# One product of 512 columns for both halves of the activations in the second layer's mixer

## The chip, the cores and the metric

The kernel runs on one core of one Trainium2 chip. The metric is the device time in microseconds (us) of one execution, as the median of the runs. Everything called an engine below belongs to that one core: TensorE (PE, with its weight loads as PEld), VectorE (DVE), ScalarE (ACT), GpSimd (POOL) and SyncE (SP), which issues the transfers.

## The reference

Two layers of an encoder on 256 tokens of width 2048, in float32. The part that matters is the first half of a layer, the mixer (cut):

```python
h = rmsnorm(x, norm_mix[l]) * (1.0 + sc_a) + sh_a
qa, ka, va, qb, kb, vb, ga, gb = split_cols(h @ w_in[l])
...
ya = window_attention(qa, ka, va, sink_a[l]) @ w_proj_a[l]
...
yb = neighbourhood_attention(qb, kb, vb, rel_bias_b[l]) @ w_proj_b[l]
merged = jax.nn.sigmoid(ga) * ya + jax.nn.sigmoid(gb) * yb
x = x + gt_a * (merged @ w_out[l])

h = rmsnorm(x, norm_ffn[l]) * (1.0 + sc_m) + sh_m
u = depthwise_conv(h @ w_up[l], conv_w[l], conv_b[l])
g, v = jnp.split(u, 2, axis=-1)
x = x + gt_m * ((jax.nn.silu(g) * v) @ w_down[l])
```

The six modulation vectors (sc_a, sh_a, gt_a and the same for the second half) are `silu(c) @ ada_w[l] + ada_b[l]`, computed in the kernel as well.

## The kernel before

**Split numbers.** TensorE multiplies in a shortened format (fp32r). To keep float32 accuracy each weight block and each activation is kept as a high half and a low half (the remainder), and a product is the sum of three: high by high, high weight by low activation, low weight by high activation.

**Blocks.** Every weight is cut into blocks of 128 by 128, and each layer's blocks stand in one stream in the order of use. Sixteen blocks are a unit: one transfer of 1 MB (`w`). A unit is split in two pieces of eight blocks (`hl_<unit>_<piece>`): ACT casts the high half (L348), then DVE subtracts to get the low half (L349). There are four buffers for pieces, and four for what the transfers bring (`raw`), which units of weights and of the modulation matrix (`aw`) share. The modulation product is done on DVE (L248), one `aw` after the other, paced by a plan against the unit number.

**Products.** `features` multiplies a row of blocks with the 16 (or 8) chunks of the activations into one PSUM tile (`ps`, four of them in turn) and then calls an evacuation. For each block `feature_block` issues, in the narrow form, three products of 256 columns (L395, L396, L397). In the wide form the two halves of the activations lie so that one access reads both (`Wide`): high weights by both halves is one product of 512 columns (L391), low weights by the high half one of 256 (L392). The sum then lies in two parts in the PSUM tile, which the evacuation adds. Before, the wide form is used in the feed-forward part only (`BOTH_HALVES`).

**The second layer's mixer, stage by stage.** After the query, key and value columns (`tokens`), with units counted from 0 in the layer: the rest of gate a (units 44 to 51, evacuation `gate_a`), projection a of the window attention's output `oA` (units 52 to 59, `proj_a`), gate b (units 60 to 75, `gate_b`), projection b of `oB` (units 76 to 83, `merge`, which also makes the halves of `merged`), the out product of `merged` (units 84 to 99, `residual`, into x). The attention heads run beside them, paced by the units. In the out product the first three output chunks share one pass over `merged` (`OUT_TURNS`), so its first three PSUM tiles are open at once; the others follow one by one.

**What sets the order.** A scheduler orders each engine's instructions when the kernel is built, so an engine's queue need not follow the code. At run time each engine takes its queue strictly in that order.

The narrow and the wide form of a block before:

```python
if isinstance(act, Wide):
    nc.tensor.matmul(ps[:], hi, act.both, start=first, stop=False)
    nc.tensor.matmul(ps[:, :S], lo, act.high, start=False, stop=last)
    return
out = ps[:, : 2 * act[0].shape[1]]
nc.tensor.matmul(out, hi, act[0], start=first, stop=False)
nc.tensor.matmul(ps[:, :S], hi, act[1], start=False, stop=False)
nc.tensor.matmul(out, lo, act[0], start=False, stop=last)
```

Of the kernel before, what the change touches and what calls it, by code (L numbers as in the profile page):

```python
# [15 lines left out]
P = 128  # L16
L = 2
D = 2048
S = 256
# [66 lines left out]
SCORES_3 = (1,)  # L86
EARLY = {1: 2}

BOTH_HALVES = (0,1)

MOVED_QK = [(), (0,1,2,8)]
QK_STEPS = 3
# [53 lines left out]
def encoder(ctx: ExitStack, tc: tile.TileContext, a: dict, out: bass.AP):  # L146
# [252 lines left out]
    class Stream:  # L399
# [54 lines left out]
        def tokens(self, h, kcs):  # L454

            pss = [mm.tile([P, 512], F32, name=f"ps{self.l}_{self.u}_t{t}", tag="mm") for t in range(2)]
            for kc in kcs:
                for _ in range(4):
                    hl, j = self.next_block()
                j -= 3  # L460
                hi, lo = (turns(hl[:, i, j * P : (j + 4) * P]) for i in range(2))
                for t, ps in enumerate(pss):
                    xh, xl = (h[kc][:, i, t * P : (t + 1) * P] for i in range(2))
                    nc.tensor.matmul(ps[:], xh, hi, start=kc == kcs[0], stop=False)  # L464
                    nc.tensor.matmul(ps[:], xh, lo, start=False, stop=False)  # L465
                    nc.tensor.matmul(ps[:], xl, hi, start=False, stop=kc == kcs[-1])  # L466
                if self.l == 0 and self.u == 1 and self.at == 4:
                    warm(WARM_ROW)
                if self.at == UB:
                    self.tick()  # L470
            return [turned_back(ps[:]) for ps in pss]

    def split(dst, src, scale=None, held=False):

        if isinstance(dst, Wide):
            hi, lo = dst.halves
            nc.scalar.copy(hi, pair(src))
            nc.vector.tensor_tensor(out=lo, in0=pair(src), in1=hi.bitcast(F32), op=ALU.subtract)
            return
        if scale is None:  # L480
            high = nc.scalar.copy(dst[:, 0], src)
            if held:
                tc.keep_in_program_order(high)
            nc.vector.tensor_tensor(out=dst[:, 1], in0=src, in1=dst[:, 0].bitcast(F32), op=ALU.subtract)
            return
        nc.scalar.activation(out=dst[:, 0], in_=src, func=AF.Copy, scale=scale)
        nc.vector.scalar_tensor_tensor(
            out=dst[:, 1], in0=src, scalar=scale, in1=dst[:, 0].bitcast(F32), op0=ALU.mult, op1=ALU.subtract
        )
# [64 lines left out]
    def normed(l, w, h, rbs):  # L554

        mod, amod = mods[l], amods[l]
        for kc in range(KC):
            t = ev.tile([P, S], F32, name="ht", tag="z")
            sh = mod[:, 3 * w * KC + kc : 3 * w * KC + kc + 1]
            nc.vector.scalar_tensor_tensor(  # L560
                out=t[:], in0=x[:, kc], scalar=amod[:, w, kc : kc + 1], in1=rbs[:], op0=ALU.mult, op1=ALU.mult
            )
            src = t[:]
            if isinstance(h[kc], Wide):
                hi, lo = h[kc].turned()
                src = src.rearrange("p (q r) -> p q r", r=2)
            else:
                hi, lo = h[kc][:, 0], h[kc][:, 1]
                if w:
                    hi, lo, src = turns(hi), turns(lo), src.rearrange("p (q r) -> p q r", r=2)  # L570
            nc.scalar.activation(out=hi, in_=src, func=AF.Identity, bias=sh)  # L571
            nc.vector.scalar_tensor_tensor(  # L572
                out=lo, in0=src, scalar=sh, in1=hi.bitcast(F32), op0=ALU.add, op1=ALU.subtract
            )
            yield
# [6 lines left out]
    class Bare:  # L582
# [42 lines left out]
        def roots(self):  # L625
            self.rbs = spread(self.rs)
            self.h = led(f"h{self.l}_{self.w}")
            if self.w and self.l in BOTH_HALVES:
                self.h = [Wide(c) for c in self.h]
            self.steps = normed(self.l, self.w, self.h, self.rbs)  # L630
            bg.add(self.steps, H_RATE[self.w])
# [89 lines left out]
    def attend(q, k, v, p, mask, scale, sink, o, rows=None):  # L721

        sc = ax.tile([P, 2, S], F32, name="sc", tag="ax")
        for t in range(2):
            for i, j in by(q):
                key = turns(k[j]) if len(q) > 1 else k[j]
                nc.tensor.matmul(sc[:, t], q[i][:, t * P : (t + 1) * P], key, start=i + j == 0, stop=(i, j) == by(q)[-1])
        m = sm.tile([P, 2], F32, name="m", tag="m")
        for t in range(2):
            nc.vector.tensor_tensor_reduce(  # L730
                out=pair(p[:, t]) if len(q) > 1 else p[:, t], in0=turned_back(sc[:, t]) if len(q) > 1 else sc[:, t],
                in1=pair(mask[:, t]) if len(q) > 1 else mask[:, t], scale=scale, scalar=-3.0e38 if sink is None else sink,
                op0=ALU.add, op1=ALU.max, accum_out=m[:, t : t + 1],
            )
        nm = sm.tile([P, 2], F32, name="nm", tag="nm")
        nc.vector.tensor_scalar(out=nm[:], in0=m[:], scalar1=-1.0, scalar2=None, op0=ALU.mult)
        den = sm.tile([P, 2], F32, name="den", tag="den")
        for t in range(2):
            nc.scalar.activation(out=p[:, t], in_=p[:, t], func=AF.Exp, bias=nm[:, t : t + 1], accum_out=den[:, t : t + 1])
        if sink is not None:  # L740
            es = sm.tile([P, 2], F32, name="es", tag="es")
            nc.scalar.activation(out=es[:], in_=nm[:], func=AF.Exp, bias=sink)
            nc.vector.tensor_tensor(out=den[:], in0=den[:], in1=es[:], op=ALU.add)
        ri = sm.tile([P, 2], F32, name="ri", tag="ri")
        nc.vector.reciprocal(out=ri[:], in_=den[:])  # L745
        for t in range(2):
            nc.scalar.activation(out=p[:, t], in_=p[:, t], func=AF.Copy, scale=ri[:, t : t + 1])
        yield
        if rows is not None:
            turned_blocks(p[:], rows(), 2)  # L750
            for _ in range(STEPS[sink is None]):
                yield
            tp = p
        else:
            tp = ax.tile([P, 2, S], F32, name="tp", tag="ax")
            for k in range(2):
                for t in range(2):
                    nc.tensor.transpose(tp[:, k, t * P : (t + 1) * P], p[:, t, k * P : (k + 1) * P], ident[:])
        pT = at.tile([P, 2, 2, S], F32R, name="pT", tag="pT", bufs=1)
        split(pT, tp[:], held=rows is not None)  # L760
        v = v()
        yield
        po = ax.tile([P, 512], F32, name="po", tag="ax")
        for i, j in by(v):
            for b in range(2):
                nc.tensor.matmul(po[:, :S], v[i][:, b], turns(pT[:, j, b]), start=i + j + b == 0, stop=i + b == 2)
        o = o()
        src, hi, lo = turned_back(po[:, :S]), pair(o[:, 0]), pair(o[:, 1])
        nc.scalar.copy(hi, src)
        nc.vector.tensor_tensor(out=lo, in0=src, in1=hi.bitcast(F32), op=ALU.subtract)  # L770

# [120 lines left out]
    for l in range(L):  # L892
# [35 lines left out]
        kTa, qTa = packs[0][:, 0:3:2], packs[0][:, 4:12]  # L928
        kvs = [None, None]

        ready, heads = [0], [0]
        oA, oB = [], []

        def head_a(i):
            g = i // (HA // GA)
            if i >= 6:
                oA.append(paired(F32R, f"oA{l}_{i}", (i - 6) * (ROW - OFF)))
            elif i % 2 == 0:
                o = place(("y0", "y1", "y2")[i // 2], 4, F32R, f"oA{l}_{i}")
                oA.extend((o[:, :2], o[:, 2:]))  # L940
            q = in_halves(qTa[:, i], f"qA{l}_{i}", "qh", l in SCORES_3)
            if i % (HA // GA) == 0:
                kvs[0] = in_halves(kTa[:, g], f"kA{l}_{g}", "kh", l in SCORES_3)
# [29 lines left out]
        def oB_of(hb):  # L973
            if hb == 0:
                o = place("a", 12, F32R, f"oB{l}_{hb}")
                oB.extend(o[:, 2 * i : 2 * i + 2] for i in range(6))
            elif hb == 6:
                oB.extend(chunks_of(sp, "b0", 6, f"oB{l}_{hb}", 2))
            return oB[hb]

        def attention():
# [28 lines left out]
        for pi, (groups, gates) in enumerate(parts):  # L1010
# [38 lines left out]
            for mo in range(BARE[0] if l else 0, KC):  # L1049

                def gate_a(ps):
                    src, to = ps, pair(ya[:, mo])
                    if pi > 0:
                        nc.vector.tensor_tensor(out=to, in0=ps, in1=to, op=ALU.add)
                        src = to
# [11 lines left out]
        for mo in range(KC):  # L1067

            def proj_a(ps):
                gated(pair(ya[:, mo]), pair(ya[:, mo]), ps)  # L1070

            st.features(oA, [proj_a])
        if l:
# [8 lines left out]

        def gate_b(mo):
            def evac(ps):
                half_tanh(pair(gb[mo]), ps)

            return evac

        for mo in range(KC):
            st.features(hs, [gate_b(mo)])  # L1090
        bg.finish(job)
        merged = led(f"merged{l}")
        for mo in range(KC):

            def merge(ps):
                z = ev.tile([P, S], F32, name="m", tag="z")
                gated(pair(z[:]), pair(gb[mo]), ps)
                nc.vector.tensor_tensor(out=z[:], in0=z[:], in1=ya[:, mo], op=ALU.add)
                split(merged[mo], z[:], 0.5)

# [195 lines left out]
```

## Time and profile before

| | |
|---|---|
| median of 3 runs (lowest to highest) | 2586.07 us (2584.91 to 2586.75) |
| the profiled execution's own time | 2584.3 us |
| its span, first to last instruction | 2581.7 us |
| mean granted TensorE clock | 0.998 |
| second layer's mixer from the rest of gate a to the end of out | about 1560.7 to 1880.8 us of the span |

The profile gives, for the whole span and for any stretch of it, how long each engine was busy; a busy PE only says that some product was in flight. Rows of instructions have the start, the duration, engine, line, operation, output and input; the time in brackets behind a row is how long the engine had stood idle before it, and what ended that. On an engine with a pipeline the next instruction starts before the last one's duration is over, so the step from start to start is what an instruction takes away from the others.

### The profile page before, as it was taken

How to read it: one execution, taken by the hardware profiler on the slowest of the kernel's cores; microseconds unless marked ns; L12 is line 12 of the kernel's file. 1: busy time of each engine (PE TensorE's matmuls, PEld its weight loads, DVE VectorE, ACT ScalarE, POOL GpSimd, SP SyncE). 2: the span in 40 equal slices, each digit the busy share in tenths (PEclk: the TensorE clock that was granted, in tenths of full speed). 3: DMA queues.
4: the chain of work that ended last, by engine and by line, in shares of the span. 5: the costliest groups of instructions: out<-in, count | busy, mean ns of one | idle time of the engine just before them, and what ended most of it. 6: DMA issues, size and time to landing. Idle time of an engine off the chain costs nothing.

```text
span 2581.7 us, 43544 instructions
## 1 busy us (share of the span) xinstructions
PE 2547.9 (99%) x17324; PEld 2378.3 (92%) x17324; DVE 2212.6 (86%) x3227; ACT 1454.8 (56%) x2432; POOL 263.1 (10%) x345
## 2 busy tenths in 40 slices
PE   8999999999999999999999999999999999999999
PEld 7999899999999999999998879999999999999998
DVE  8998998998998899799987778879889987766775
ACT  5445765456663665466565566654576546644663
POOL 0001100000000000000003668730000000000000
PEclk9999999999999999999999999999999999999999
DMA  9998789986778778777767667778848775555554
GB/s 370 352 349 306 263 299 356 335 315 227 259 292 307 258 285 297 291 279 279 281 226 271 262 229 264 258 284 332 309 175 294 291 295 197 206 201 197 204 202 147
DMA packets 102158, 699.97 MB, mean 271 GB/s; under 512 B 12866, under 2 KB 15170, under 8 KB 18114
## 3 DMA queue, kind: packets, MB, share of 16 engines
q1 hardware_dynamic: 101954, 697.20, 73.0%
q8 instruction: 135, 2.21, 0.3%
q14 instruction: 69, 0.56, 0.1%
HBM read 695.06 MB, written 2.10 MB: 270 GB/s over the span
## 4 chain that ended last, share of the span: by engine, by line
PE 70%; DVE 14%; DMA 6%; ACT 4%; issue 4%; POOL 2%; SPq 0%; ACTq 0%; DVEq 0%; POOLq 0%
PE ps L391 31%; PE ps L392 15%; DVE hl L349 5%; PE ps L397 5%; PE ps L395 5%; PE ps L396 5%; DVE aw L248 4%; DMA aw<-in_aw 3%; PE ps_t L465 2%; PE ps_t L464 2%; PE ps_t L466 2%; ACT hl L348 2%; DMA w<-in_ws 2%; POOL p L320 1%; DVE x L1108 1%
## 5 line engine op out<-in xcount | busy, mean ns | idle before, releaser
L349 DVE TENSOR_TENSOR hl<-w,hl 128x1024 fp32r<-128x1024 f32 x928 | 1130.3, 1224 | 215.4 <-ACT hl L348 213.1
L348 ACT CAST hl<-w 128x1024 fp32r<-128x1024 f32 x928 | 964.7, 1046 | 587.0 <-PE ps L392 253.8
L391 PE MATMUL ps<-h,hl 128*128 128x512 f32 x2432 | 796.8, 382 | 0.0
L392 PE MATMUL ps<-h,hl 128*128 128x256 f32 x2432 | 662.9, 273 | 0.0
L391 PEld LDWEIGHTS ps<-h,hl 128*128 128x128 f32 x2432 | 459.7, 189 | 64.0
L392 PEld LDWEIGHTS ps<-h,hl 128*128 128x128 f32 x2432 | 466.9, 192 | 0.0
L248 DVE CUSTOM_DVE_ANT_0 aw<-aw,cact,ab 128x2048 f32<-128x2048 f32 x189 | 443.8, 2349 | 14.0 <-DMA aw<-in_aw 13.4
L395 PE MATMUL ps<-h,hl 128*128 128x256 f32 x896 | 247.3, 276 | 1.9 <-DVE ri L745 0.8
L397 PE MATMUL ps<-h,hl 128*128 128x256 f32 x896 | 245.9, 276 | 0.6 <-DVE hl L349 0.6
L396 PE MATMUL ps<-h,hl 128*128 128x256 f32 x896 | 246.4, 275 | 0.0
L465 PE MATMUL ps_t<-hl,h 128*128 128x512 f32 x576 | 220.4, 383 | 4.8 <-DVE hl L349 4.5
L464 PE MATMUL ps_t<-hl,h 128*128 128x512 f32 x576 | 217.7, 383 | 3.8 <-ACT h L571 2.4
L466 PE MATMUL ps_t<-hl,h 128*128 128x512 f32 x576 | 219.0, 381 | 0.0
L395 PEld LDWEIGHTS ps<-h,hl 128*128 128x128 f32 x896 | 171.9, 192 | 3.1 <-PE ps L397 0.9
L396 PEld LDWEIGHTS ps<-h,hl 128*128 128x128 f32 x896 | 172.0, 192 | 0.4 <-DVE h L572 0.2
L397 PEld LDWEIGHTS ps<-h,hl 128*128 128x128 f32 x896 | 171.6, 192 | 0.8 <-DVE hl L349 0.8
L391 PE MATMUL ps<-act_o,hl 128*128 128x512 f32 x512 | 170.5, 382 | 0.0
L1135 DVE SCALAR_TENSOR_TENSOR u<-both,cw,u 128x255 f32<-128x255 f32 x304 | 146.0, 480 | 3.8
L397 PE MATMUL ps<-merged,hl 128*128 128x256 f32 x512 | 140.8, 276 | 3.5 <-DVE hl L349 3.5
L395 PE MATMUL ps<-merged,hl 128*128 128x256 f32 x512 | 140.7, 275 | 0.4 <-ACT hl L348 0.4
L396 PE MATMUL ps<-merged,hl 128*128 128x256 f32 x512 | 140.6, 275 | 0.0
L392 PE MATMUL ps<-act_o,hl 128*128 128x256 f32 x512 | 139.6, 273 | 0.0
(242 smaller groups left out, 4867.6 us busy)
## 6 DMA issues: line engine op xcount, KB each, us to landing
w<-in_ws SPq DMA_DIRECT2D x463, 1024.0 KB, 4.9
aw<-in_aw SPq DMA_DIRECT2D x189, 1024.0 KB, 5.0
p<-in_bias SPq DMA_DIRECT2D x16, 256.0 KB, 4.9
x<-in_xT SPq DMA_DIRECT2D x4, 512.0 KB, 5.4
aw_o<-in_aw SPq DMA_DIRECT2D x2, 1024.0 KB, 12.8
out<-x SPq DMA_DIRECT2D x16, 128.0 KB, 2.2
w<-in_ws SPq DMA_DIRECT2D x2, 512.0 KB, 12.1
aw_b<-in_aw SPq DMA_DIRECT2D x1, 1024.0 KB, 17.9
```

The lines of the kernel that those rows point to most:

```text
L248: product = nc.vector.tensor_tensor_reduce(out=raw[:], in0=raw[:], in1=cact[:], scale=1.0, scalar=ab[:, i : i + 1], op0=ALU.mult, op1=ALU. ...
L348: nc.scalar.copy(hl[:, 0], r)
L349: nc.vector.tensor_tensor(out=hl[:, 1], in0=r, in1=hl[:, 0].bitcast(F32), op=ALU.subtract)
L391: nc.tensor.matmul(ps[:], hi, act.both, start=first, stop=False)
L392: nc.tensor.matmul(ps[:, :S], lo, act.high, start=False, stop=last)
L395: nc.tensor.matmul(out, hi, act[0], start=first, stop=False)
L396: nc.tensor.matmul(ps[:, :S], hi, act[1], start=False, stop=False)
L397: nc.tensor.matmul(out, lo, act[0], start=False, stop=last)
L464: nc.tensor.matmul(ps[:], xh, hi, start=kc == kcs[0], stop=False)
L465: nc.tensor.matmul(ps[:], xh, lo, start=False, stop=False)
L466: nc.tensor.matmul(ps[:], xl, hi, start=False, stop=kc == kcs[-1])
L1135: nc.vector.scalar_tensor_tensor(out=u[:, to], in0=ps[:, of], scalar=w[:, j : j + 1], in1=u[:, to], op0=ALU.mult, op1=ALU.add)
```

## The change

In the second layer (`BOTH_MIXED = (1,)`) the normalised input `h`, the attention outputs `oA` and `oB` and `merged` are laid out as `Wide`. All products of `features` in that mixer behind the bare part of gate a take the wide form: 8 rows of gate a, 16 of projection a, 16 of gate b, 16 of projection b and 16 of out, with 16, 8, 16, 8 and 16 blocks a row. A new helper `joined` adds the two parts of a sum (a copy on ACT, an addition on DVE) ahead of each evacuation; `residual` already takes a list and adds the two parts to x one after the other. `tokens` reads the high and low halves from the new places, with the same products.

```diff
-BOTH_HALVES = (0,1)
+BOTH_HALVES = (0, 1)
+BOTH_MIXED = (1,)
...
+        if isinstance(dst, Wide) and scale:
+            hi, lo = dst.halves
+            nc.scalar.activation(out=hi, in_=pair(src), func=AF.Copy, scale=scale)
+            nc.vector.scalar_tensor_tensor(
+                out=lo, in0=pair(src), scalar=scale, in1=hi.bitcast(F32), op0=ALU.mult, op1=ALU.subtract
+            )
+            return
...
-            if self.w and self.l in BOTH_HALVES:
+            if self.l in (BOTH_HALVES if self.w else BOTH_MIXED):
                 self.h = [Wide(c) for c in self.h]
...
+        def wide(chunks):
+
+            return [Wide(c) for c in chunks] if l in BOTH_MIXED else chunks
+
+        def joined(ps):
+
+            if not isinstance(ps, list):
+                return ps
+            z = ev.tile([P, S], F32, name="both", tag="z")
+            nc.scalar.copy(pair(z[:]), ps[1])
+            nc.vector.tensor_tensor(out=pair(z[:]), in0=ps[0], in1=pair(z[:]), op=ALU.add)
+            return pair(z[:])
...
-                    src, to = ps, pair(ya[:, mo])
+                    src, to = joined(ps), pair(ya[:, mo])
...
-                gated(pair(ya[:, mo]), pair(ya[:, mo]), ps)
+                gated(pair(ya[:, mo]), pair(ya[:, mo]), joined(ps))
...
-                half_tanh(pair(gb[mo]), ps)
+                half_tanh(pair(gb[mo]), joined(ps))
...
-        merged = led(f"merged{l}")
+        merged = wide(led(f"merged{l}"))
...
-                gated(pair(z[:]), pair(gb[mo]), ps)
+                gated(pair(z[:]), pair(gb[mo]), joined(ps))
```

How it moves instructions. In the rows below a PSUM tile's name has the number of units fetched and the block within the unit at which it begins: `ps_83_16` is the tile whose products read the piece `hl_83_0`, `ps_84_8` the next, which reads `hl_83_1`, and `ps_84_16_0` to `ps_84_16_2` are the first three tiles of the out product. `m` is the merge's gated sum, `both` the new joined sum, `bare_1_a` and `bare_1_b` one-column entries for the next part.

The first place is DVE's queue at the end of projection b. Before:

```order
L497 SCALAR_TENSOR_TENSOR m<-gb_0_17397,ps_83_8_0_18987 128x256
L349 TENSOR_TENSOR hl_83_1_19026<-w_83_19021,hl_83_1_19026 128x1024
L487 SCALAR_TENSOR_TENSOR merged_18519<-m,merged_18519 128x256
L1098 TENSOR_TENSOR m<-m,ya_13577 128x256
L248 ISA aw_71_19083,mod_9378<-aw_71_19083,cact,ab_9379 128x2048
L248 ISA mod_9378 128x1
L487 SCALAR_TENSOR_TENSOR merged_18519<-m,merged_18519 128x256
L497 SCALAR_TENSOR_TENSOR m<-gb_1_17398,ps_83_16_0_19020 128x256
L257 SCALAR_TENSOR_TENSOR amod_9383<-mod_9378,nrm_9381 128x1
L497 SCALAR_TENSOR_TENSOR m<-gb_1_17398,ps_84_8_0_19058 128x256
L1098 TENSOR_TENSOR m<-m,ya_13577 128x256 x2
L349 TENSOR_TENSOR hl_84_0_19106<-w_84_19104,hl_84_0_19106 128x1024
```

And now, up to the instruction that frees the same tile `ps_83_16`:

```order
L951 TENSOR_TENSOR both<-ps_82_16_0_18497,both 128x256
L627 TENSOR_TENSOR bare_1_a<-mod_9378,bare_1_a 128x1 x2
L505 SCALAR_TENSOR_TENSOR m<-gb_0_17213,both 128x256
L627 TENSOR_TENSOR bare_1_a<-mod_9378,bare_1_a 128x1 x2
L1121 TENSOR_TENSOR m<-m,ya_13577 128x256
L350 TENSOR_TENSOR hl_85_1_18677<-w_85_18672,hl_85_1_18677 128x1024
L479 SCALAR_TENSOR_TENSOR merged_18127<-m,merged_18127 128x2x128 x2
L951 TENSOR_TENSOR both<-ps_83_8_0_18530,both 128x256
L627 TENSOR_TENSOR bare_1_b_18623<-mod_9378,bare_1_b_18623 128x1 x2
L505 SCALAR_TENSOR_TENSOR m<-gb_0_17213,both 128x256
L627 TENSOR_TENSOR bare_1_b_18623<-mod_9378,bare_1_b_18623 128x1
L951 TENSOR_TENSOR both<-ps_83_16_0_18558,both 128x256
```

The tile `ps_83_16` was freed ahead of the piece `hl_84_0`; now the pieces `hl_84_0` to `hl_85_1`, `aw_72` and eight one-column entries stand ahead of it.

The second place is PE's queue at the start of the out product. Before, the first blocks of its three tiles in turn:

```order
L395 MATMUL ps_84_16_0_19101<-merged_18519,hl_84_0_19106 128x256
L396 MATMUL ps_84_16_0_19101<-merged_18519,hl_84_0_19106 128x256
L395 MATMUL ps_84_16_1_19102<-merged_18519,hl_84_0_19106 128x256
L396 MATMUL ps_84_16_1_19102<-merged_18519,hl_84_0_19106 128x256
L395 MATMUL ps_84_16_2_19103<-merged_18519,hl_84_0_19106 128x256
L396 MATMUL ps_84_16_2_19103<-merged_18519,hl_84_0_19106 128x256
L397 MATMUL ps_84_16_0_19101<-merged_18519,hl_84_0_19106 128x256
```

And now, from the eighth block of the first tile to the first block of the third:

```order
L392 MATMUL ps_84_16_0_18629<-merged_18127,hl_85_0_18674 128x512
L393 MATMUL ps_84_16_0_18629<-merged_18127,hl_85_0_18674 128x256
L392 MATMUL ps_84_16_0_18629<-merged_18127,hl_85_1_18677 128x512
L393 MATMUL ps_84_16_0_18629<-merged_18127,hl_85_1_18677 128x256
L392 MATMUL ps_84_16_1_18630<-merged_18127,hl_84_0_18634 128x512
L393 MATMUL ps_84_16_1_18630<-merged_18127,hl_84_0_18634 128x256
```

Nine blocks of the first tile, out of the pieces `hl_84_0` to `hl_85_1`, now come ahead of the first block of the second tile; three blocks of the second tile follow, and then the third's.

The third place is DVE's queue at the end of projection a, where the heads of the second attention write `oB`. Before:

```order
L326 STREAM_TRANSPOSE packB_1_14136<-p 128x2x256
L349 TENSOR_TENSOR hl_59_1_17339<-w_59_17334,hl_59_1_17339 128x1024
L248 ISA aw_56_17330,mod_9378<-aw_56_17330,cact,ab_9379 128x2048
L248 ISA mod_9378 128x1
L497 SCALAR_TENSOR_TENSOR ya_13577<-ya_13577,ps_58_16_0_17212 128x256
L349 TENSOR_TENSOR hl_60_0_17402<-w_60_17400,hl_60_0_17402 128x1024
```

And now:

```order
L951 TENSOR_TENSOR both<-ps_59_8_0_17077,both 128x256
L780 TENSOR_TENSOR oB_0_16725<-po,oB_0_16725 128x2x128
L492 TENSOR_TENSOR pT<-p,pT 128x512
L492 TENSOR_TENSOR vB_3_17106<-packB_0_14135,vB_3_17106 128x256
L492 TENSOR_TENSOR qB_6_17147<-packB_1_14136,qB_6_17147 128x256
L492 TENSOR_TENSOR kB_6_17150<-packB_1_14136,kB_6_17150 128x256
L505 SCALAR_TENSOR_TENSOR ya_13577<-ya_13577,both 128x256
L350 TENSOR_TENSOR hl_60_0_17218<-w_60_17216,hl_60_0_17218 128x1024
```

The head's five instructions, which stood behind `hl_60_1`, now stand ahead of `hl_60_0`, together with joined sums.

More of the change, by code (lines that the diff above doesn't have):

```diff
@@ L462, in tokens @@
                 for t, ps in enumerate(pss):
-                    xh, xl = (h[kc][:, i, t * P : (t + 1) * P] for i in range(2))
+                    xh, xl = (h[kc].halves[i][:, t] if isinstance(h[kc], Wide) else h[kc][:, i, t * P : (t + 1) * P] for i in range(2))
                     nc.tensor.matmul(ps[:], xh, hi, start=kc == kcs[0], stop=False)
@@ L563, in normed @@
             src = t[:]
-            if isinstance(h[kc], Wide):
+            if isinstance(h[kc], Wide) and w == 0:
+                (hi, lo), src = h[kc].halves, pair(src)
+            elif isinstance(h[kc], Wide):
                 hi, lo = h[kc].turned()
@@ L767, in attend @@
         o = o()
-        src, hi, lo = turned_back(po[:, :S]), pair(o[:, 0]), pair(o[:, 1])
+        src, (hi, lo) = turned_back(po[:, :S]), o.halves if isinstance(o, Wide) else (pair(o[:, 0]), pair(o[:, 1]))
         nc.scalar.copy(hi, src)
@@ L936, in head_a @@
             if i >= 6:
-                oA.append(paired(F32R, f"oA{l}_{i}", (i - 6) * (ROW - OFF)))
+                oA.extend(wide([paired(F32R, f"oA{l}_{i}", (i - 6) * (ROW - OFF))]))
             elif i % 2 == 0:
                 o = place(("y0", "y1", "y2")[i // 2], 4, F32R, f"oA{l}_{i}")
-                oA.extend((o[:, :2], o[:, 2:]))
+                oA.extend(wide([o[:, :2], o[:, 2:]]))
             q = in_halves(qTa[:, i], f"qA{l}_{i}", "qh", l in SCORES_3)
@@ L975, in oB_of @@
                 o = place("a", 12, F32R, f"oB{l}_{hb}")
-                oB.extend(o[:, 2 * i : 2 * i + 2] for i in range(6))
+                oB.extend(wide([o[:, 2 * i : 2 * i + 2] for i in range(6)]))
             elif hb == 6:
-                oB.extend(chunks_of(sp, "b0", 6, f"oB{l}_{hb}", 2))
+                oB.extend(wide(chunks_of(sp, "b0", 6, f"oB{l}_{hb}", 2)))
             return oB[hb]
```

## The prediction

> **What bounds the kernel now.** I read the page first, then a table by stage, then single rows.
>
> ```profile
> span 2581.7 us, 43544 instructions
> ...
> PE 2547.9 (99%) x17324; PEld 2378.3 (92%) x17324; DVE 2212.6 (86%) x3227; ACT 1454.8 (56%) x2432; POOL 263.1 (10%) x345
> ...
> PE 70%; DVE 14%; DMA 6%; ACT 4%; issue 4%; POOL 2%; SPq 0%; ACTq 0%; DVEq 0%; POOLq 0%
> ```
>
> PE is bound nearly everywhere, DVE stands close behind. The averages hide that the stages differ. By stage (gate a's rest, projection a, gate b, projection b, out, the start of the feed-forward part, and a stretch of it that is wide already):
>
> ```profile
> core 0: us, PE busy (x) PEld busy (x) DVE busy (x) ACT busy (x) POOL busy (x), PEclk, DMA share, GB/s
> 1560.70:1607.60 46.90, 46.90 (x423) 46.90 (x422) 41.54 (x66) 32.17 (x71) 41.48 (x61) 1.00 0.70 251
> 1607.60:1654.40 46.80, 46.80 (x422) 46.80 (x421) 43.50 (x75) 27.72 (x50) 36.70 (x53) 1.00 0.76 274
> 1654.40:1745.80 91.40, 90.83 (x814) 90.64 (x813) 71.78 (x94) 48.21 (x81) 41.62 (x54) 1.00 0.73 277
> 1745.80:1791.40 45.60, 43.39 (x387) 43.01 (x386) 45.49 (x74) 22.12 (x34) 0.00 (x0) 1.00 0.87 331
> 1791.40:1880.80 89.40, 86.55 (x770) 85.97 (x769) 78.94 (x119) 45.47 (x75) 0.00 (x0) 1.00 0.83 304
> 1880.80:1950.00 69.20, 68.13 (x595) 66.97 (x595) 60.57 (x106) 51.61 (x100) 0.70 (x1) 1.00 0.51 185
> 1950.00:2050.00 100.00, 100.00 (x613) 91.99 (x612) 94.17 (x133) 61.04 (x93) 0.00 (x0) 1.00 0.81 299
> ```
>
> In projection b DVE is busy 45.49 of 45.60 us and PE is not: there DVE is the bound. In projection a DVE has 3.3 us free, in out 10.5.
>
> ```profile
> DVE aw L248 <- DMA aw<-in_aw: 5.9, 5, 2.2
> ...
> PE ps L397 <- DVE hl L349: 4.7, 4, 1.7
> ```
>
> These two waits are of projection b and out together: PE stops four times for the split weights, and of DVE's free time 5.9 us is waiting for the modulation's transfers.
>
> **What a block saves on PE.** The narrow products stand at even steps; first and last of 177 rows in gate b, then first and last of 173 rows in the wide stretch:
>
> ```profile
> 1719.52 0.28 PE L397 MATMUL ps<-h,hl 128*128 128x256 f32 x1
> ...
> 1739.17 0.28 PE L396 MATMUL ps<-h,hl 128*128 128x256 f32 x1
> ```
>
> ```profile
> 1999.33 0.38 PE L391 MATMUL ps<-h,hl 128*128 128x512 f32 x1
> ...
> 2027.50 0.38 PE L391 MATMUL ps<-h,hl 128*128 128x512 f32 x1
> ```
>
> Narrow: 19.65 us / 176 steps = 111.65 ns a product, three a block = 335.0 ns. Wide: 28.17 / 172 = 163.8 ns, two a block = 327.6 ns. The columns are the same 768; what goes is 7.4 ns a block. The change touches 8 x 16 + 16 x 8 + 16 x 16 + 16 x 8 + 16 x 16 = 896 blocks: 6.6 us at most, of which gate a 0.9, projection a 0.9, gate b 1.9, projection b 0.9, out 1.9. The Trainium skill (TensorE: Matmul & The Clock Gate, section Back-to-back issue gap) speaks against even this: a warm product takes its columns at 2.4 GHz plus about 2.5 ns, so that by estimate a narrow block would be 327.5 ns, a wide one 325.0, and the 896 blocks would save 2.2 us, with which the sum below would stand 4.4 us higher. The narrow rows disagree with it, by 111.65 against 109.2 ns.
>
> **What it adds.** 56 joined sums (8 + 16 + 16 + 16), each a copy on ACT and an addition on DVE, and 16 more additions into x in out. The wide stretch has the same pair:
>
> ```profile
> L1157 ACT COPY both<-ps 128x256 f32<-128x256 f32 x16 | 5.9, 369 | 11.2 <-PE ps L392 10.9
> ```
>
> ```profile
> L1158 DVE TENSOR_TENSOR both<-ps,both 128x256 f32<-128x256 f32 x16 | 6.7, 418 | 0.9 <-ACT both L1157 0.9
> ```
>
> On DVE the duration isn't the price; the step to the next start is:
>
> ```profile
> 1780.69 1.21 DVE L349 TENSOR_TENSOR hl<-w,hl 128x1024 fp32r<-128x1024 f32 x1
> 1781.82 0.41 DVE L1098 TENSOR_TENSOR m<-m,ya 128x256 f32<-128x256 f32 x1
> 1782.16 2.34 DVE L248 CUSTOM_DVE_ANT_0 aw<-aw,cact,ab 128x2048 f32<-128x2048 f32 x1
> 1784.43 0.08 DVE L248 DVE_READ_ACCUMULATOR2_ANT mod<- 128x1 f32 x1
> 1784.43 0.41 DVE L487 SCALAR_TENSOR_TENSOR merged<-m,merged 128x256 fp32r<-128x256 f32 x1
> 1784.77 0.41 DVE L497 SCALAR_TENSOR_TENSOR m<-gb,ps 128x256 f32<-128x256 f32 x1
> 1785.10 1.21 DVE L349 TENSOR_TENSOR hl<-w,hl 128x1024 fp32r<-128x1024 f32 x1
> ```
>
> ```profile
> 1835.39 0.48 DVE L1108 SCALAR_TENSOR_TENSOR x<-ps,mod,x 128x256 f32<-128x256 f32 x1
> 1835.78 1.22 DVE L349 TENSOR_TENSOR hl<-w,hl 128x1024 fp32r<-128x1024 f32 x1
> ```
>
> So a split piece takes 1.14 us, a 256-column operation 0.335, a modulation product 2.27, an addition into x 0.39. The change gives DVE 56 x 0.335 + 16 x 0.39 = 25.0 us more, in 320 us in which it has 38.8 free (the sum over the five stages).
>
> ACT gets 56 x 0.37 = 20.7 us; in its fullest stage it is busy 32.17 of 46.90, so I price the copies at nothing. What stands behind them in ACT's queue is the next cast; a tanh that waits for DVE's sum could hold that up, and on DVE the sum waits for the copy, with the splits that PE needs behind it. In the wide stretch DVE waits 0.9 us for 16 copies; 56 of them at this rate are 3.2 us, the upper end; the lower is 0, which I take, since PE was never idle there. POOL's queue is unchanged, and on SP's three bias transfers for the heads each go ahead of one neighbour: nothing, since only their places in a full queue change. The products of query, key and value read the same 128 columns from other places: nothing, between 0 and 0.
>
> **Gate a, projection a, gate b.** PE gains 0.9 + 0.9 + 1.9 = 3.7 us. In gate a DVE's 8 sums (2.7 us) and the shorter stage (0.9) fit into 5.4 us free: no cost; without that cover 2.7. In gate b 5.4 + 1.9 fit into 19.6 free: no cost. In projection a 5.4 + 0.9 don't fit into 3.3: DVE is 3.0 us short.
>
> ```profile
> ACT hl L348 <- PE ps L397: 13.2, 10, 1.6
> ...
> DVE packB L326 <- ACT p L747: 2.0, 3, 0.7
> ```
>
> These waits are projection a's. ACT is held ten times because PE has not freed a piece yet, so the splits run ahead as far as four buffers allow, and some shortage could be drawn from that lead. But the third place of the order shows a head's five instructions now ahead of `hl_60_0`, which draws on the same lead. Bounds: 0 (the lead takes it all) and 6.3 (none of the free time is usable, because it is waiting for ACT's softmax, as 2.0 us of it is). I take 3.0, the stage's own balance. Sum of the three stages: -3.7 + 3.0 = -0.7.
>
> **Projection b and the start of out.** This is where it is decided. DVE works without a pause from the first `aw` to the instruction that frees `ps_83_16`:
>
> ```profile
> 1746.35 2.35 DVE L248 CUSTOM_DVE_ANT_0 aw<-aw,cact,ab 128x2048 f32<-128x2048 f32 x1
> ...
> 1791.32 0.40 DVE L497 SCALAR_TENSOR_TENSOR m<-gb,ps 128x256 f32<-128x256 f32 x1
> ```
>
> Its queue before holds there 13 pieces (14.8 us), 7 modulation products (15.9), 43 operations of 256 columns (14.4) and small ones (0.3): 45.4, and the rows give 45.3. So the prices hold. Its queue now holds from the same `aw` to the same tile 17 pieces (19.4), 8 modulation products (18.2), 55 operations (18.4) and small ones (1.1, a one-column entry at the 0.08 of the row of that width above): 57.1 us. PE can't go past a tile that isn't freed. By the same count `ps_82_8` is free at 49.8, `ps_82_16` at 53.1, `ps_83_8` at 56.2. The last tile of projection b starts at 49.8; nine blocks of out's first tile (as the order shows) fill 53.1 to 56.1, three of the second to 57.2, and the other 36 of the first pass take 36 x 0.3276 = 11.8: it ends at 69.0.
>
> ```profile
> 1791.38 0.28 PE L395 MATMUL ps<-merged,hl 128*128 128x256 f32 x1
> ...
> 1793.98 0.38 PE L397 MATMUL ps<-merged,hl 128*128 128x256 f32 x1 [1.72 <-DVE hl L349]
> ```
>
> Before, the pass starts here and takes 48 x 0.335 + the stop of 1.72 = 17.8 us, to 1809.2, or 62.8 after the same `aw`. The pass ends 6.2 us later, and one sum now stands ahead of that `aw`: 0.3. Bounds: 0 if the lead absorbed it, which the 45.3 us without a pause make unlikely, and 9.7 if PE waits for the third tile before it does anything of out (57.1 + 48 x 0.3276 = 72.8). I take 6.5, since the order says what PE finds to do.
>
> **The rest of out.** 208 blocks at 7.4 ns: -1.5. DVE's 16 x 0.39 = 6.2 us and the shorter stage (1.9) fit into 10.5 free, by 2.4, if DVE can work through its waits for transfers; it then has no lead left. What it owes, the next stage repays (60.57 of 69.20). I price it at nothing; the upper end is a rival.
>
> **Sum:** -0.7 + 6.5 - 1.5 = +4.3 us. The profiled execution took 2584.3 us, 1.8 below the median of the runs shown; from the median, 2586.07 + 4.3 = 2590.4 us.
>
> **Rivals.** *Out becomes DVE's as well* (slower). Place: out behind its first pass. DVE 78.94 + 6.2 + the 5.9 of waits for transfers = 91.0 us against 89.4 - 1.9 = 87.5: 3.5 us more, 2593.9. It decides once more than 2.4 of those 5.9 us stay. For it: the stage moves 304 GB/s already, and a transfer's buffer is freed by the same late DVE. Against: a later DVE finds transfers landed.
>
> *The sums are hidden* (faster). DVE's lead takes projection a's shortage and projection b's, and PE's 6.6 us come through: 2579.5. For it: in the wide stretch DVE is busy 94.17 of 100 with PE full. Against: projection b has 0.1 us free and gets 16 sums.
>
> *No gain in the products* (slower). If a 512-column product cost two narrow ones, the blocks would save nothing: 2590.4 + 6.6 = 2597.0. Against it stand 327.6 ns a block in the wide stretch. The Trainium skill's gap, cited above, is a milder form of this: 2594.8.
>
> **How the numbers follow.** A measurement of this kernel can tell about 0.2%, 5.2 us, from no change. The forecast has 0.58: its own range, 2586 to 2595, lies on both sides of 2591.3, 0.42 below and 0.16 above. Out DVE-bound 0.25, no gain 0.03, hidden sums 0.14 (0.11 faster by over 0.2%, 0.03 within). So faster 0.11, same 0.45, slower 0.44. The range goes from 2581 (the lower ends of both DVE terms, 3.0 and 6.5 less) to 2599 (projection a's 3.3 more, out's 3.5, and some of ACT's 3.2).
>
> **What would show it.** PE rows: 896 fewer, at 327.6 ns a block where nothing waits. Projection b: DVE still full, PE's stops for PSUM tiles or splits longer by 5 to 7 us. Projection a: new stops of PE around its end. Rest of out: about 68 us for 208 blocks, or 3 more if DVE is full. I am wrong if DVE's queue has pauses in projection b, if its lead is larger than the waits of ACT tell, or if PE's steps elsewhere change.

## The result and the profile after

| | before | after |
|---|---|---|
| median (lowest to highest), the two kernels on the same chip | 2586.66 us (2584.86 to 2591.89) | 2595.78 us (2590.15 to 2600.3) |
| ratio, with its 95% interval | | 1.0031 (1.0021 to 1.0040) |
| the profiled execution: own time, span | 2584.3, 2581.7 us | 2596.82, 2594.7 us |

The change made the kernel 9.1 us slower, by its interval 5.4 to 10.3 us; the forecast was 4.3. In the parts of the page on busy time and on the chain of work that ended last, PE keeps its busy time with 896 products fewer, and DVE's share of the chain rises from 14% to 16%:

```profile
span 2594.7 us, 41858 instructions
...
PE 2547.6 (98%) x16428; PEld 2351.7 (91%) x16428; DVE 2236.6 (86%) x3299; ACT 1472.5 (57%) x2488; POOL 260.1 (10%) x345
...
PE 73%; DVE 16%; ACT 3%; issue 3%; POOL 3%; DMA 1%; DVEq 0%; ACTq 0%; POOLq 0%
```

The table by stage, in the columns of the prediction's: the rest of gate a, projection a, gate b, projection b, out.

```profile
1566.40:1612.40 46.00, 46.00 (x295) 42.64 (x294) 42.60 (x72) 33.79 (x78) 40.40 (x59) 1.00 0.70 253
1612.40:1660.40 48.00, 46.23 (x294) 42.46 (x293) 47.24 (x88) 32.01 (x67) 33.89 (x53) 1.00 0.71 255
1660.40:1751.00 90.60, 88.80 (x556) 81.74 (x555) 79.04 (x114) 52.92 (x97) 42.44 (x56) 1.00 0.76 284
1751.00:1805.70 54.70, 43.89 (x259) 38.52 (x257) 54.67 (x92) 26.80 (x50) 0.00 (x0) 1.00 0.87 326
1805.70:1893.80 88.10, 86.17 (x512) 78.36 (x513) 81.36 (x133) 47.30 (x76) 0.00 (x0) 0.98 0.78 278
```

Before, these stages took 46.9 + 46.8 + 91.4 + 45.6 + 89.4 = 320.1 us; now 46.0 + 48.0 + 90.6 + 54.7 + 88.1 = 327.4. Projection b alone is 9.1 us longer, the other four together 1.8 us shorter. In projection b DVE is busy 54.67 of 54.70 us and PE 43.89: DVE was the bound of this stage already and now has more to do. The waits of PE in this stage name it:

```profile
PE ps L392 <- DVE both L951: 6.6, 5, 1.9
...
PE ps L392 <- DVE amod L258: 3.8, 2, 1.9
```

Five times PE stands because a PSUM tile is not free until DVE has made its joined sum. (In the second row the instruction named is a one-column entry that stands in the same full queue.) The three marks of the prediction's count, in the rows of DVE: the first `aw`, the instruction that frees `ps_83_16`, and the first addition into x, which comes at about the end of out's first pass.

```profile
1752.36 2.34 DVE L249 CUSTOM_DVE_ANT_0 aw<-aw,cact,ab 128x2048 f32<-128x2048 f32 x1
...
1809.05 0.42 DVE L951 TENSOR_TENSOR both<-ps,both 128x256 f32<-128x256 f32 x1
...
1821.43 0.87 DVE L1131 SCALAR_TENSOR_TENSOR x<-ps,mod,x 128x256 f32<-128x256 f32 x2
```

From 1752.36 to the next start after the second row, 1809.38, are 57.0 us (counted: 57.1); to the third row 69.1 (counted: 69.0). By PE's rows the first product behind the pass starts at 1821.6.

The profiled execution of after is 13.0 us longer in its span, not 7.3. The other 5.7 us arise ahead of gate a's rest (it starts at 1566.4 instead of 1560.7), in code whose instructions did not change, nearly all of them in the first layer; 3.1 of them lie in its gate b, projection b and out, which took 223.7 us before and 226.8 after, and 222.4 to 228.3 in all the kernels below that leave these stages alone. That is how single executions scatter here. So I read effects from the five stages and the verdict from the medians. What fills the gap between 7.3 us in one execution and 9.1 in the medians stays open; the interval holds both.

### The profile page after: what moved, and what is told of

Same layout as the page of the kernel before. It is cut to its first block, busy times and chain, and to the rows that moved or that the text cites. A ratio compares the mean times of both kernels' runs of the same rounds, so it can differ in the third digit from the quotient of the medians.

```text
span 2594.7 us, 41858 instructions
## 1 busy us (share of the span) xinstructions
PE 2547.6 (98%) x16428; PEld 2351.7 (91%) x16428; DVE 2236.6 (86%) x3299; ACT 1472.5 (57%) x2488; POOL 260.1 (10%) x345
## 4 chain that ended last, share of the span: by engine, by line
PE 73%; DVE 16%; ACT 3%; issue 3%; POOL 3%; DMA 1%; DVEq 0%; ACTq 0%; POOLq 0%
PE ps L392 34%; PE ps L393 17%; DVE hl L350 6%; PE ps L398 4%; PE ps L396 4%; PE ps L397 4%; DVE aw L249 4%; PE ps_t L465 2%; PE ps_t L466 2%; PE ps_t L467 2%; ACT hl L349 1%; DMA aw<-in_aw 1%; POOL p L321 1%; POOL packA L321 1%; DVE x L1131 1%
## 5 line engine op out<-in xcount | busy, mean ns | idle before, releaser
L392 PE MATMUL ps<-h,hl 128*128 128x512 f32 x2816 | 923.2, 382 | 0.0
L393 PE MATMUL ps<-h,hl 128*128 128x256 f32 x2816 | 767.7, 273 | 1.8 <-DVE hl L350 1.8
L392 PEld LDWEIGHTS ps<-h,hl 128*128 128x128 f32 x2816 | 532.3, 189 | 73.8
L393 PEld LDWEIGHTS ps<-h,hl 128*128 128x128 f32 x2816 | 540.7, 192 | 2.1 <-DVE hl L350 2.1
L396 PE MATMUL ps<-h,hl 128*128 128x256 f32 x512 | 141.7, 278 | 1.9 <-DVE ri L755 0.8
L397 PE MATMUL ps<-h,hl 128*128 128x256 f32 x512 | 140.8, 276 | 0.0
L398 PE MATMUL ps<-h,hl 128*128 128x256 f32 x512 | 140.2, 276 | 0.0
L1131 DVE SCALAR_TENSOR_TENSOR x<-ps,mod,x 128x256 f32<-128x256 f32 x240 | 113.0, 482 | 21.9 <-PE ps L393 20.1
L466 PEld LDWEIGHTS ps_t<-hl,h 128*128 128x128 f32 x576 | 109.4, 190 | 23.5 <-DVE hl L350 8.6
L465 PEld LDWEIGHTS ps_t<-hl,h 128*128 128x128 f32 x576 | 109.2, 190 | 20.2 <-ACT h L581 3.3
L1180 ACT COPY both<-ps 128x256 f32<-128x256 f32 x152 | 56.3, 371 | 123.5 <-PE ps L393 122.4
L467 PEld LDWEIGHTS ps_t<-hl,h 128*128 128x128 f32 x576 | 109.6, 190 | 15.4
```

## The experiments

The theory: the loss sits in DVE's queue in projection b, and the products do gain what the rows of the wide stretch say. For each kernel below, the length of the five stages in its profiled execution, by the first and last product of each stage (gate a here from the end of the query, key and value columns, 1.6 us earlier than in the table above; out includes the step over from projection b), and the ratio to the kernel before:

| kernel | gate a | proj. a | gate b | proj. b | out | sum | ratio (95% interval) |
|---|---|---|---|---|---|---|---|
| before | 48.5 | 46.8 | 91.4 | 45.5 | 89.4 | 321.6 | |
| after | 47.5 | 47.9 | 90.7 | 54.0 | 88.7 | 328.8 | 1.0031 (1.0021 to 1.0040) |
| nar_oB | 47.5 | 47.9 | 90.7 | 47.8 | 89.7 | 323.6 | 1.0001 (0.9990 to 1.0012) |
| only_oB | 48.4 | 46.8 | 90.9 | 54.9 | 88.7 | 329.7 | 1.0027 (1.0018 to 1.0037) |
| sums_only | 48.5 | 46.7 | 91.1 | 54.5 | 87.6 | 328.4 | 1.0050 (1.0035 to 1.0066) |
| products_only | 48.5 | 46.8 | 90.7 | 46.6 | 87.2 | 319.8 | 0.9999 (0.9987 to 1.0011) |
| ada_moved | 47.5 | 48.6 | 88.9 | 41.8 | 87.9 | 314.7 | 1.0027 (1.0016 to 1.0038) |
| before_ada | 48.5 | 46.8 | 90.5 | 42.8 | 85.8 | 314.4 | 1.0017 (1.0008 to 1.0027) |
| only_out | 48.4 | 46.8 | 90.6 | 45.7 | 88.3 | 319.8 | 0.9998 (0.9987 to 1.0008) |
| only_oA | 48.5 | 46.7 | 93.3 | 46.5 | 90.8 | 325.8 | 1.0013 (1.0004 to 1.0022) |
| ff_before | 48.4 | 46.8 | 90.7 | 42.8 | 85.8 | 314.5 | 0.9963 (0.9950 to 0.9975) |
| ff_after | 47.5 | 47.9 | 90.8 | 41.8 | 88.9 | 316.9 | 0.9985 (0.9975 to 0.9996) |
| ff2_before | 48.5 | 46.8 | 90.5 | 42.8 | 85.8 | 314.4 | 1.0002 (0.9993 to 1.0011) |
| ff2_after | 47.5 | 46.0 | 89.9 | 41.8 | 83.8 | 309.0 | 0.9993 (0.9983 to 1.0003) |

Two things limit this table. Every kernel has its own order from the scheduler, so a row shows an amount of work together with the order that goes with it. And in four of the profiled executions there is, within the five stages, a stretch of 3.4 us in which the granted TensorE clock (PEclk in the rows, 1.00 at full speed) was 0.50: in out in after and nar_oB, in projection b in only_oB and sums_only. Half of 3.4 us, 1.7, is the most that it can have cost each of these sums.

### Projection b alone, with and without its parts

**nar_oB**: the changed kernel without the change in projection b.

```diff
-                oB.extend(wide([o[:, 2 * i : 2 * i + 2] for i in range(6)]))
+                oB.extend(o[:, 2 * i : 2 * i + 2] for i in range(6))
...
-                oB.extend(wide(chunks_of(sp, "b0", 6, f"oB{l}_{hb}", 2)))
+                oB.extend(chunks_of(sp, "b0", 6, f"oB{l}_{hb}", 2))
```

> The changed kernel with the narrow form kept for projection b alone (oB laid out as before, 16 joined sums and 128 wide blocks fewer). Theory: the loss sits in DVE's full queue of projection b; without the 16 sums there it goes back, so that from the changed kernel's 9.1 us over the kernel before some 7 go: 0 to +3 us against the kernel before, and projection b takes 45 to 48 us again instead of 54.7. Rival (the loss comes from the sums as such, through ACT's copies and the waits between ACT and DVE in every stage): 56 sums share 9.1 us, 40 of them are left, so +6 to +7 us.

**only_oB**: the reverse; `wide` is left out for `h`, `oA` and `merged`.

> The kernel before with the wide form in projection b alone. Theory: DVE has 16 x 0.335 = 5.4 us more to do in a stage in which it is busy 45.49 of 45.60 us, and its order changes as well: +5 to +7 us against the kernel before, projection b together with the first pass of out 5 to 7 us longer. Rival (the loss is shared by all sums): 16 of 56 sums, +2.6 us. Second rival (DVE's debt from gate a, projection a and gate b is what projection b pays): with these stages as before, under +2 us.

**sums_only**: the kernel before, with a sum of the same size ahead of each merge (the copy is times 0, so the value stays).

```diff
-                gated(pair(z[:]), pair(gb[mo]), ps)
+                w = ev.tile([P, S], F32, name="both", tag="z")
+                nc.scalar.activation(out=pair(w[:]), in_=ps, func=AF.Copy, scale=0.0)
+                nc.vector.tensor_tensor(out=pair(w[:]), in0=ps, in1=pair(w[:]), op=ALU.add)
+                gated(pair(z[:]), pair(gb[mo]), pair(w[:]))
```

> The kernel before, all products narrow, with a copy on ACT (times 0) and an addition on DVE ahead of each of the 16 evacuations of projection b: the cost of the sums without the gain of the products. Theory: the same +5 to +7 us as with the wide products in projection b, and 0.9 more for the products' gain (128 x 7.4 ns) that is missing: +6 to +8. Rival (the wide tiles of 512 columns or the new layout of oB cost the time): under +2.

**products_only**: only_oB with `gated(pair(z[:]), pair(gb[mo]), ps[0])`, so no copy and no addition; the result lacks the second part of each sum.

> The kernel before with the wide products in projection b, but without the joined sums: the second half of each sum (high weight by low activation) is left out of the result there. Theory: DVE's and ACT's work is that of before, so only the products' gain is left: 128 x 7.4 ns = -0.9 us if PE is the bound there, and nearer to 0 because DVE is: -1 to 0. Rival (the wide products or the layout of oB cost the time): +3 or more.

Measured, as medians beside that of the kernel before (2587.11 us): nar_oB 2586.77, only_oB 2593.32, sums_only 2598.86, products_only 2586.29. Projection b's row in the table by windows of each, in this order:

```profile
1748.60:1796.40 47.80, 43.85 (x386) 43.12 (x385) 46.38 (x74) 22.44 (x35) 0.00 (x0) 1.00 0.87 323
```

```profile
1749.50:1804.40 54.90, 45.11 (x258) 39.72 (x257) 53.90 (x89) 26.35 (x46) 0.00 (x0) 0.97 0.91 339
```

```profile
1751.10:1805.60 54.50, 46.31 (x386) 44.98 (x384) 52.71 (x84) 25.55 (x44) 0.00 (x0) 0.97 0.92 339
```

```profile
1742.90:1789.50 46.60, 42.75 (x257) 38.34 (x256) 45.85 (x76) 22.41 (x38) 0.00 (x0) 1.00 0.88 327
```

With the sums DVE has 53 to 54 us to do in this stage and the stage takes 54.5 to 54.9, whether the products are wide (x258) or narrow (x386). Without them it takes 46.6 to 47.8, again for both. (The 0.97 in the second and third row is the stretch at half pace named above; the difference of some 7 to 8 us is far more than its 1.7.) So the sums cost the time, not the 512-column products or the layout of `oB`. Without projection b the change costs nothing that can be told (nar_oB), and projection b alone costs 0.27%, nearly the whole of the change's 0.31%. Both rivals of only_oB fall: a third of the sums costs far more than a third of the loss, and the debt from earlier stages isn't needed.

My expectation for sums_only spoke of 16 evacuations, but the edited line runs in both layers. Its five stages of the second layer are 6.8 us longer than before, within the expected 6 to 8; the first layer's gate b, projection b and out take 231.3 us, 7.6 more than the 223.7 before. Together that is 14.4 us in this execution, with a stretch at half pace in each of the two places, beside 11.8 in the medians.

### Taking other work out of DVE's queue

**ada_moved** and **before_ada**: the changed kernel and the kernel before, with the eight modulation products of projection b done earlier.

```diff
-ADA_PLAN_1 = [(8, 132), (76, 160), (84, 168), (99, 176), ...
+ADA_PLAN_1 = [(8, 132), (44, 156), (60, 162), (76, 168), (84, 168), (99, 176), ...
```

> The changed kernel with the eight modulation products of projection b moved ahead: the plan's units 44, 60, 76 and 84 now stand at 156, 162, 168 and 168 products in place of 147, 153, 160 and 168, so most of them fall into the query, key and value columns, where DVE is busy some 19 of 25 us. Theory (DVE's queue is the bound of projection b): 8 x 2.27 = 18.2 us leave a stage in which DVE was full for 54.7; PE's 43.9 us and its own pace become the bound again, so projection b falls to 44 to 46 us, and the kernel stands at -4 to +1 us against the kernel before, 8 to 10 us under the changed one. Rival (PE waits in projection b for ACT's copies and the latency of each evacuation, not for DVE's throughput): the stage stays above 52 us, the kernel at +6 to +9.

> The kernel before with the same eight modulation products moved ahead, the control to the one above. Theory: projection b is DVE's already (45.49 of 45.60 us busy, PE 43.39), so the kernel gains the 2.2 us in which PE stood there and not much more, as 128 narrow blocks need 42.9 us: -1 to -3 us. Rival (moving them costs in the stages that take them): +1 to +4.

Measured: 2591.96 and 2589.97 us, beside 2584.87 for the kernel before. Projection b's row of each:

```profile
1755.10:1796.90 41.80, 41.80 (x257) 38.50 (x256) 38.76 (x68) 25.34 (x44) 0.00 (x0) 1.00 0.61 215
```

```profile
1760.00:1802.80 42.80, 42.80 (x386) 42.80 (x385) 37.65 (x61) 22.30 (x36) 0.00 (x0) 1.00 0.61 219
```

In the stage itself the theory holds as sharply as it can: without the eight products DVE has 38.76 us to do, PE never stops, and the wide form takes 41.8 against 42.8 us. Its 128 blocks save 1.0 us; 128 x 7.4 ns is 0.9. The totals missed my expectation, since I had taken DVE's idle time in the query, key and value columns (5 to 7 of every 25 us) to be free. These columns with the bare part of gate a took 264.2 and 265.3 us instead of 253.9 (after) and 253.7 (before). The waits of PE for splits there, in after and in ada_moved:

```profile
PE ps_t L466 <- DVE hl L350: 4.1, 4, 2.8
```

```profile
PE ps_t L466 <- DVE hl L350: 9.3, 6, 5.4
```

These waits are 5.2 us of the 10.3 that ada_moved took longer than after there; waits of PE for ACT's casts are 2.0 more. Part of the rest is the granted clock: it was 0.97 over these columns, with PE busy 249.5 of 264.2 us, and 0.99 in after, with PE busy 245.5 of 253.9. The longest of the stops shows that DVE's idle time there is waiting, not room. DVE stands for the root that POOL works out for the query's norm, with the next split behind it in the queue; the waits of DVE for it, in after and in ada_moved:

```profile
DVE qn L671 <- POOL qrs L543: 13.9, 3, 5.9
```

```profile
DVE qn L671 <- POOL qrs L543: 17.8, 5, 6.2
```

In the longest of these waits PE stops for 2.8 us in after and for 5.4 in ada_moved. That the moved products take the time in which DVE would have run more splits ahead of such a wait is the likely reason; no run isolates it.

### Projection a and out alone

**only_out** and **only_oA**: `wide` for `merged` alone, and for `oA` alone.

> The kernel before with the wide form in the out product alone (merged laid out wide, 256 blocks, no joined sum, 16 more additions into x). Theory: DVE's 6.2 us more fit into its free time of out, so the products' gain comes through: -1.9 us, out 87.5 us instead of 89.4. Rival (out becomes DVE's, as the rival of the prediction has it, or a stop of PE at its end costs what the products gain): out 89 to 91 us, 0 to +2 against the kernel before.

> The kernel before with the wide form in projection a alone (oA laid out wide, 16 joined sums, 128 blocks). Theory: DVE has 5.4 us more to do in a stage with 3.3 free; part of the shortage is drawn from its lead: projection a 47 to 49 us instead of 46.8, and the kernel at 0 to +3 against the kernel before. Rival (the sums are hidden by the lead): projection a 45.9, -1 us.

Measured: 2585.20 and 2588.64 us, beside 2584.87. only_out lies between the two expectations: out is 1.1 us shorter in its profiled execution, and the ratio can't tell -1.9 from 0. only_oA is slower by 3.4 us (1.0 to 5.7), somewhat more than expected, and the time is not where I looked for it. Projection a and gate b in its table by windows:

```profile
1612.20:1658.90 46.70, 46.15 (x293) 42.41 (x292) 45.59 (x86) 31.52 (x65) 32.57 (x51) 1.00 0.71 256
1658.90:1752.20 93.30, 91.11 (x812) 90.71 (x812) 75.42 (x99) 48.32 (x82) 42.23 (x56) 1.00 0.75 280
```

Projection a itself stays at 46.7 us: its shortage is drawn from DVE's lead. The debt is paid in gate b (93.3, where the kernels with narrow products and an old projection a show 90.5 to 91.4) and, less clearly, in projection b and out (1.0 and 1.4 us over before).

### A place where DVE has room

**ff_before** and **ff_after**: the same eight products moved into the first layer's feed-forward part instead, in the kernel before and in the changed one.

```diff
-ADA_PLAN_0 = [..., (108, 80), (231, 132)]
-ADA_PLAN_1 = [(8, 132), (76, 160), (84, 168), (99, 176), ...
+ADA_PLAN_0 = [..., (108, 80), (231, 140)]
+ADA_PLAN_1 = [(8, 140), (76, 168), (84, 168), (99, 176), ...
```

> The kernel before, with eight of the modulation products of projection b moved not into the query, key and value columns but into the first layer's feed-forward part (its plan ends at 140 in place of 132, and the second layer's plan runs 140, 168, 168, 176 in place of 132, 160, 168, 176): there DVE is busy 40 to 47 of every 50 us, with some 50 us free in 500, and needs 18.2 more. Theory: the 7.2 us that the second layer's mixer won when they left projection b come through, since nothing is lost where they go: -4 to -8 us against the kernel before. Rival (they cost about as much anywhere): 0 to +4.

> The changed kernel with the same plan. Theory: projection b falls to 42 us, and the kernel stands at -4 to -8 us against the kernel before, within 2 us of the same plan without the change: what the products gain in gate a, gate b and projection b (some 3.5 us) is lost to DVE in projection a and out. Rival (with projection b free, the change's 6.6 us come through in full): -11 to -14.

**ff2_before** and **ff2_after**: sixteen products moved there, and none left in projection a, projection b and out.

```diff
+ADA_PLAN_0 = [..., (108, 80), (231, 148)]
+ADA_PLAN_1 = [(8, 148), (44, 163), (52, 166), (60, 166), (76, 176), (99, 176), ...
```

> The kernel before with sixteen modulation products moved into the first layer's feed-forward part, so that projection a, projection b and out have none of them and gate b some ten. Theory: PE has no stop left in the five stages, which the control with eight had reached already (314.4 us, all of them busy): the same -4 to -8 us, if 36.4 us fit into the first layer's feed-forward part; 0 to 2 worse if not.

> The changed kernel with sixteen modulation products moved as in the one before it. Theory (only DVE's queue keeps the products' gain from coming through): with projection a, projection b and out free of them, DVE has room for all 56 sums and 16 additions, and the five stages take 308 to 311 us against 314.4, so the change makes this kernel 3 to 6 us faster than the same plan without it, at -8 to -13 against the kernel before. Rival (a wide block gains nothing beside the sums, because the evacuation is longer or the order worse): no faster than the same plan without the change.

Measured, beside 2586.68 us: ff_before 2578.53, ff_after 2583.53, ff2_before 2589.84, ff2_after 2585.62. A stretch of the first layer's feed-forward part in before, ff_before and ff2_before:

```profile
1000.00:1240.00 240.00, 240.00 (x1468) 220.66 (x1467) 210.10 (x301) 130.32 (x194) 0.00 (x0) 1.00 0.77 285
```

```profile
1000.00:1240.00 240.00, 240.00 (x1468) 220.69 (x1468) 218.70 (x308) 132.64 (x194) 0.00 (x0) 1.00 0.80 299
```

```profile
1000.00:1240.00 240.00, 239.68 (x1458) 219.31 (x1457) 221.81 (x311) 127.58 (x192) 0.00 (x0) 1.00 0.83 310
```

Eight products are hidden there: the same 1468 products of PE in the same time. With sixteen PE has to wait for splits; from the first layer's out to the second layer's first product it takes 709.0 us instead of 696.9. PE's waits there are 8.0 us instead of 0.8; the other 5 us lie in time that the profile counts as busy, and stay open. So ff_before came out as expected: it is faster than the kernel before by 0.25 to 0.50%, and so than the changed one as well. ff2_before missed: the five stages were as short as forecast, and the price of moving took the 7.2 us back and left no change that can be told.

The pair ff2 is the cleanest test of the products. A window of out behind its first pass, in ff2_before and in ff2_after:

```profile
1819.30:1872.00 52.70, 52.70 (x474) 52.70 (x473) 36.91 (x52) 28.57 (x41) 0.00 (x0) 1.00 0.55 198
```

```profile
1819.30:1870.00 50.70, 50.70 (x312) 46.69 (x311) 41.37 (x63) 28.66 (x42) 0.00 (x0) 1.00 0.56 201
```

The two windows do not hold the same blocks; they show that PE never stops in either. The five stages take 314.4 us narrow and 309.0 wide: -1.0, -0.8, -0.6, -1.0 and -2.0, where 7.4 ns a block gives -0.9, -0.9, -1.9, -0.9 and -1.9. Only gate b falls short; PE stops there for 0.7 us in ff2_after (it is busy 89.19 of 89.90 us), which leaves 0.6 us without a cause. In total 5.4 of the 6.6 us come through, and the medians of the pair differ by 4.2. The Trainium skill's rule that the prediction weighed (TensorE: Matmul & The Clock Gate, Back-to-back issue gap), which the page gives for a single product by itself, would by estimate have given 2.2 us for the 896 blocks; the trace, with 5.4, doesn't agree. With only eight products moved, the change still costs 2.4 us in the five stages and 5.0 in the medians (ff_after against ff_before). I had expected the two within 2 us; with projection b free, projection a and out are still short of DVE.

## Why the prediction was right, and where not

The forecast, 4.3 us slower, had the sign, the place and the mechanism, and half of the measured 9.1; the measured median of 2595.8 us lies just above the range of the forecast's own case, 2586 to 2595, and within the whole range. In the profiled executions the steps come to -0.9 + 0.4 + 6.9 + 0.9 = +7.3 us, and 2.4 of the 3.0 us that the forecast lacks are in the last of them, the rest of out. The further 1.8 us of the medians are not explained. By its steps:

**Products.** 7.4 ns a block: shown by ff2 (5.4 of 6.6 us, of which gate b's stop explains 0.7) and by projection b in ada_moved and before_ada (1.0 us).

**Gate a, -0.9.** 46.9 to 46.0: right.

**Projection a, +2.1, and gate b, -1.9.** Measured +1.2 and -0.8. The sum of the two, +0.4 against +0.2, is right, but the cover that was named for gate b's sums, 19.6 us of free time, was not the point: DVE enters gate b late, since projection a has used up its lead, and PE loses 1.8 us there. only_oA shows that debt by itself. The step that failed is to have put the shortage into the stage that makes it; that the sum came out right all the same is partly luck.

**Projection b and out's first pass, +6.5.** By PE's rows it took 63.7 us from the end of gate b to the end of the first pass before (1745.8 to 1809.5; the 1809.2 of the prediction was worked out) and 70.6 now (1751.0 to 1821.6): +6.9. DVE's queue was counted to 0.1 us; the difference is that the first `aw` starts 1.4 us behind the end of gate b, where 0.8 was reckoned (0.55 before and one sum of 0.3). The upper bound of this term was added up wrongly: 72.8 - 62.8 is 10.0, not 9.7.

**The rest of out, -1.5.** This is the term that was mis-sized: 71.35 us before, 72.25 after, so +0.9. 208 blocks at 0.335 us are 69.68, so 1.7 us were lost before; 208 at 0.3276 are 68.14, so 4.1 are lost now. In both kernels they are lost near the end. The last 15 us of out, before and after:

```profile
1865.70:1880.70 15.00, 13.87 (x122) 13.48 (x121) 11.48 (x19) 7.45 (x13) 0.00 (x0) 1.00 0.77 301
```

```profile
1878.70:1893.70 15.00, 13.07 (x68) 11.32 (x67) 11.16 (x20) 7.55 (x13) 0.00 (x0) 0.89 0.65 227
```

The greater part of the loss is a stop, about 2.6 us with the slow start behind it. At the same block PE lost 1.7 us before, so the stop grew by 0.9. First ACT's rows of after there, then PE's:

```profile
1874.76 1.05 ACT L349 CAST hl<-w 128x1024 fp32r<-128x1024 f32 x1
1878.96 0.42 ACT L523 ACTIVATE sq<-x 128x256 f32<-128x256 f32 x1 [3.15 <-DVE x L1131]
1879.28 0.50 ACT L622 ACTIVATE bare_y<-x,amod 128x256 fp32r<-128x256 f32 x1
1879.68 1.03 ACT L349 CAST hl<-w 128x1024 fp32r<-128x1024 f32 x1
```

```profile
1879.23 0.38 PE L392 MATMUL ps<-merged,hl 128*128 128x512 f32 x1
1880.76 0.48 PE L392 MATMUL ps<-merged,hl 128*128 128x512 f32 x1 [1.15 <-ACT hl L349]
1882.02 0.38 PE L393 MATMUL ps<-merged,hl 128*128 128x256 f32 x1 [0.78 <-DVE hl L350]
1882.24 0.38 PE L392 MATMUL ps<-merged,hl 128*128 128x512 f32 x1
...
1883.49 0.63 PE L392 MATMUL ps<-merged,hl 128*128 128x512 f32 x1
1883.92 0.42 PE L393 MATMUL ps<-merged,hl 128*128 128x256 f32 x1
1884.13 0.63 PE L392 MATMUL ps<-merged,hl 128*128 128x512 f32 x1
```

ACT stands 3.15 us for DVE's late addition into x, with the cast of the next piece two places behind; then PE waits for that cast and for its low half. I had priced ACT's queue at nothing because ACT is seldom busy; what counts is what it stands in front of. The other 1.5 us are the granted clock: shortly after the stop a block takes 0.64 us (1883.49 to 1884.13) instead of 0.33. The rival "out becomes DVE's as well" is half right: DVE does set the end, but its waits for transfers fell from 5.9 to 2.0 us, as the prediction's argument against it said, and the loss came by a stop and the clock.

```profile
DVE aw L249 <- DMA aw<-in_aw: 2.0, 2, 1.4
```

Whether every execution has this dip is not shown; among the other profiled ones with `merged` wide, nar_oB has it (0.89) and only_out, ada_moved, ff_after and ff2_after don't. In ff2_after, with DVE relieved, the stop is gone as well.

**The other rivals.** The sums are hidden: refuted in projection b by sums_only, and true only where DVE is relieved (ff2). No gain in the products: refuted by ff2.

## What to carry to other kernels

Cost an operation on the second-busiest engine stage by stage: 16 times 0.335 us of DVE, put into the one stage where DVE was full already, made the kernel 6.2 us slower (only_oB against before), and cost little where DVE had room or a lead. Before trading PE time for DVE time, look at what else stands in that stage's queue and can go elsewhere: moving eight modulation products to a stage with room was worth 0.25 to 0.50% here, as much as all of the wide products could give at best (6.6 us) or more. Free time in a table of averages is room only if nothing urgent stands behind it in the queue: the same eight products cost nothing in one stage with idle DVE time and 10 us, part of it by the clock, in another.

## What was not expected of the hardware

The granted clock fell to half pace after a stop of only 1.15 + 0.78 us with one product between, and came back after 3.4 us (1882.9 to 1886.3), at a price of some 1.5 us, beside 2.6 for the stop itself. In this window of after, behind the stop, PE is busy throughout and the granted clock is 0.50:

```profile
1884.00:1886.00 2.00, 2.00 (x8) 1.72 (x7) 0.81 (x3) 0.00 (x0) 0.00 (x0) 0.50 0.60 98
```

The Trainium skill (TensorE: Matmul & The Clock Gate, HAM oscillation) gives as the abstract rule that idle gaps of over about 3.4 us are to be avoided; this stop was shorter. Nor is a dip certain after one: in only_out the same stop, 1.14 + 0.78 us at the same block, is followed by a granted clock of 1.00. In projection b of after PE stood for 10.8 us in all, 1.9 at most at a time, at a granted clock of 1.00 throughout, and in projection b of only_oB a stop of the same 1.9 us is followed by 3.4 us at half pace (1776.5 to 1779.9). What decides it is not shown.
